# Two fp32 parts of a weight chunk in one tile, a wide product for v, and three full accumulator banks for each branch product in a hybrid encoder trunk

## The chip, the cores and the metric

The kernel runs on one core of a Trainium2 chip. The metric is the device time of one execution in microseconds (us). The kernel before has a median of 2629.47 us over 3 runs (2629.2 to 2629.55). The engines are called by the profile's short names: PE is the matrix engine's multiplications and PEld its weight loads, DVE the vector engine, ACT the scalar engine, POOL the GpSimd engine, SP the engine that issues most transfers. PSUM is the memory that PE writes its sums to; one of its banks holds 512 fp32 numbers in each of 128 partitions.

## The reference

The reference is an encoder trunk of two layers on 256 tokens of width 2048, in fp32:

```python
h = rmsnorm(x, norm1_g[l])
z = h @ w_in[l]               # conformer 2*512 | short conv 3*512 | q,k,v 3*768 | gates 3*2048
y_a = conformer_conv(z) @ w_a_out[l]          # 512 -> 2048
y_b = short_gated_conv(z) @ w_b_out[l]        # 512 -> 2048
y_c = dilated_attention(q, k, v) @ w_c_out[l] # 256 -> 2048
g_a, g_b, g_c = split(sigmoid(zg + b_gate[l]))
m = g_a * y_a + g_b * y_b + g_c * y_c
x = x + m @ w_o[l]
x = x + (silu(h2 @ w_ffn_gate[l]) * (h2 @ w_ffn_up[l])) @ w_ffn_down[l]   # h2 = rmsnorm(x, norm2_g[l])
```

The attention has 12 heads in 3 groups with dilations 1, 4 and 16; the conformer branch has a depthwise convolution with 31 taps and a layer norm. After the last layer comes one more RMSNorm.

## The kernel before, in words

**Every product is made of two parts.** Each fp32 operand is split into a rounded part (type fp32r) and the rest of it: x = hi + lo. A product is hi·hi + lo·hi + hi·lo. In the activations' tiles, 128 x 512, the high part fills the left 256 columns and the rest the right 256. `product` (lines 175 to 193) therefore multiplies the high part of a weight block with all 512 columns at once (line 189, a "wide" product) and the weight's rest with the left 256 (line 190, a "narrow" one). The left and the right half of the bank then have to be added: `joined` (lines 195 to 203) copies the right half to SBUF on ACT (line 198) and adds the two on DVE (line 202).

**Weights come in chunks of 128 x 1024** (1280 for the branches' output weights, 1408 for the second FFN matrix; these are cut in two pieces). There are 1072 pieces. For each piece ACT makes the rounded part `wh` (line 144) and DVE the rest `wl` (line 145). Raw chunks, `wh` and `wl` have three buffers each in the pool `wp`; a piece is split while the two ahead of it are still to be multiplied. A piece of 1024 columns holds 8 weight blocks, so 8 wide and 8 narrow products.

**v is the exception.** For v the activations are the stationary operand and the weights move: lines 499 to 501 make three narrow products for each of the 16 blocks of the depth, 2 halves of the tokens, 3 head groups and 2 layers. Each accumulator `pv` uses 256 of its bank's 512 columns, and one ACT copy (line 506) takes it to SBUF.

**The branch products** (lines 600 to 614) are another: for each of the 16 column blocks j, ten weight blocks make y_a (4), y_b (4) and y_c (2) with three narrow products each (lines 610 to 612). y_a and y_b share one bank (`pab`), y_c has half of another (`pc`). `branch_out` multiplies them with the gates on DVE straight from PSUM (lines 619 to 621), sums them, and splits the sum for the following product with w_o. All accumulators, of every product, come from the pool `pa`, which has five banks; a second pool `px` of three banks serves the attention's and norms' small products.

**What sets the order.** The program is recorded in the order of the Python code, and a list scheduler with its own model of times then places each instruction in the queue of its engine; each engine runs its queue in order. The splits of weight pieces have a higher priority than the rest (`SOONER`). The work beside the products (convolution taps on DVE, layer norm, attention) waits in the queue `beside`, and `some` lets a part of it be recorded after each piece. The layer norm of the conformer branch needs two sums over four tiles on POOL (`ln_sum`, lines 429 to 431), a small product `mu` on PE, and four SiLUs on ACT (line 453); the sigmoids (line 636), SiLUs and exponentials (line 537) each need their function table loaded on ACT when the one before was another. The attention's results `csp` are two tiles; each branch's y_c needs both. The first branch products are recorded after gate product 14, the second after gate product 16 of a layer's 48.

Of the kernel before, what the change touches and what calls it, by code (L numbers as in the profile page):

```python
# [16 lines left out]
P = 128  # L17
# [32 lines left out]
def trunk(ctx, tc, xt, wf, win, wv, wy, wo, wgu, wd, cst, fin, dist, out):  # L50
# [39 lines left out]
    def acc(name):  # L90
        return pa.tile([P, 2 * S], F32, tag="acc", name=name)
# [44 lines left out]
    def split_to(pi):  # L136
        while state["split"] < min(pi, len(pieces)):
            i = state["split"]
            ci, a, b = pieces[i]
            load_to(ci + 1)  # L140
            wh = wp.tile([P, 1024], F32R, tag="wh", name="wh")
            wl = wp.tile([P, 1024], F32R, tag="wl", name="wl")
            with tc.high_priority(SOONER if state["use"] >= 2 else 0):
                nc.scalar.copy(wh[:, :b - a], raws[ci][:, a:b])  # L144
                nc.vector.tensor_sub(wl[:, :b - a], raws[ci][:, a:b], wh[:, :b - a].bitcast(F32))  # L145
            split[i] = (wh, wl)
            if b == chunks[ci][1]:
                del raws[ci]
            state["split"] += 1
# [13 lines left out]
    def drain():  # L163
        some(1e9)

    def piece():
        i = state["use"]
        load_to(min(len(chunks), pieces[min(i + 1, len(pieces) - 1)][0] + AHEAD_LOAD))
        split_to(i + AHEAD_SPLIT)
        state["use"] += 1  # L170
        _, a, b = pieces[i]
        wh, wl = split.pop(i)
        return wh, wl, (b - a) // P

    def product(dst, xs, whole=False, budget=0.9):

# [161 lines left out]
    for k in range(KD):  # L338
        norm.take(k)
        if k < KD - 3:  # L340
            wh, wl = tile2r("wh"), tile2r("wl")
        else:

            wh, wl = (wp.tile([P, 1024], F32R, tag=t, name=t) for t in ("wh", "wl"))
        for a, b in CUTS.get(k, [(0, HEAD * P)]):
            nc.scalar.copy(wh[:, a:b], fw[k][:, a:b])
            nc.vector.tensor_sub(wl[:, a:b], fw[k][:, a:b], wh[:, a:b].bitcast(F32))
        for n, ps in enumerate(heads):
            nc.tensor.matmul(ps, wh[:, n * P:(n + 1) * P], turned(norm.xs[k]), start=k == 0, stop=False)
        for n, ps in enumerate(heads):  # L350
            nc.tensor.matmul(ps[:, :S], wl[:, n * P:(n + 1) * P], turned(norm.xs[k][:, :S]), start=False, stop=k == KD - 1)
# [38 lines left out]
    for l in range(DEPTH):  # L390
# [96 lines left out]
        h = norm.later  # L487
        v = [[None] * 2 for _ in range(NG)]
        for g in range(NG):
            pv = [acc("v")[:, :S] for _ in range(2)]  # L490
            k = 0
            while k < KD:
                wh, wl, nk = piece()
                for i in range(nk // 2):
                    w = slice(i * S, (i + 1) * S)
                    for b in range(2):
                        hi = h[k][:, b * P:(b + 1) * P]
                        lo = h[k][:, S + b * P:S + (b + 1) * P]
                        nc.tensor.matmul(pv[b], hi, turned(wh[:, w]), start=k == 0, stop=False)
                        nc.tensor.matmul(pv[b], lo, turned(wh[:, w]), start=False, stop=False)  # L500
                        nc.tensor.matmul(pv[b], hi, turned(wl[:, w]), start=False, stop=k == KD - 1)
                    k += 1
                some(0.9)
            for b in range(2):
                v[g][b] = vp.tile([P, S], F32, tag=f"v{g}{b}", name="v")
                nc.scalar.copy(v[g][b], pv[b])

# [83 lines left out]
        gates, m = {}, []  # L593

        def branch(j):
            ps = branch_products()
            with tc.high_priority(2 * SOONER if j == KD - 1 else 0):
                branch_out(j, ps)

        def branch_products():  # L600
            ys = asp + bsp + csp
            pab, pc = acc("yab"), acc("yc")[:, :S]
            dsts = [pab[:, :S]] * 4 + [pab[:, S:]] * 4 + [pc] * 2
            first, final = (0, 4, 8), (3, 7, 9)
            k = 0
            while k < 10:
                wh, wl, nk = piece()
                for i in range(nk):
                    w = slice(i * P, (i + 1) * P)
                    nc.tensor.matmul(dsts[k], wh[:, w], turned(ys[k][:, :S]), start=k in first, stop=False)  # L610
                    nc.tensor.matmul(dsts[k], wh[:, w], turned(ys[k][:, S:]), start=False, stop=False)  # L611
                    nc.tensor.matmul(dsts[k], wl[:, w], turned(ys[k][:, :S]), start=False, stop=k in final)
                    k += 1
            return pab, pc

        def branch_out(j, ps):
            pab, pc = ps
            ga, gb, gc = gates.pop(j)
            nc.vector.tensor_mul(ga, ga, pab[:, :S])
            nc.vector.tensor_mul(gb, gb, pab[:, S:])  # L620
            nc.vector.tensor_mul(gc, gc, pc)
            nc.vector.tensor_add(ga, ga, gb)
            nc.vector.tensor_add(ga, ga, gc)
            mj = tile2r("mj")
            halves(mj, ga)
            m.append(mj)
# [166 lines left out]
```

## Time and profile before

| what | us |
|---|---|
| median of the runs | 2629.47 |
| the profiled execution | 2629.61 |
| its span, from the first to the last instruction | 2627.8 |
| PE busy | 2609.8 |
| DVE busy | 1895.1 |
| ACT busy | 1440.4 |
| POOL busy | 117.5 |

The granted clock of PE is 0.998. PE is busy nearly everywhere, so a duration is best read as the distance between the starts of two matmuls: the records overlap, since a matmul of 256 columns is shown with 0.28 us and the next one starts 0.11 us after it. The stages of the first layer stand in the trace in this order: the conformer's inputs, q and k up to 114.4 us, v from there to about 147 us, the short convolution's inputs, the gates from 210.4 us, the branch products among them from 302 us.

### The profile page before, as it was taken

The numbers are of one execution on the slowest core, as the hardware profiler recorded it, in microseconds if no ns is written. First come the engines' busy times: TensorE is split into PE (matmuls) and PEld (weight loads), VectorE is DVE, ScalarE is ACT, GpSimd is POOL, SyncE is SP. The second block draws the span as 40 slices with busy tenths as digits, with TensorE's granted clock in tenths as the row PEclk, the third lists the DMA queues.
The fourth block names the chain that finished last, engine by engine and source line by source line (L and its number), as shares of the span: only waits on it lengthen the run. The fifth ranks groups of instructions, "written<-read, shape, count | busy, mean of one in ns | idle before, by whom it ended". The sixth has DMA issues, their size and how long they took to land.

```text
span 2627.8 us, 42886 instructions
## 1 busy us (share of the span) xinstructions
PE 2609.8 (99%) x16740; PEld 2411.8 (92%) x16740; DVE 1895.1 (72%) x2903; ACT 1440.4 (55%) x2063; POOL 117.5 (4%) x92
## 2 busy tenths in 40 slices
PE   9999999999999999999999999999999999999998
PEld 8998899999999999999999989999999999999997
DVE  8998566678766666666899966666787666666665
ACT  6547655555645545445664565555565454454555
POOL 2001000011000000000102000000200000000002
PEclk9999999999999999999999999999999999999999
DMA  6665466666666666666566555666666666666664
GB/s 239 202 201 186 149 207 197 204 200 200 201 201 201 202 200 202 205 197 204 194 201 200 191 183 171 204 198 199 204 199 202 199 201 205 197 201 203 199 204 154
DMA packets 137581, 519.36 MB, mean 198 GB/s; under 512 B 15520, under 2 KB 17184, under 8 KB 137376
## 3 DMA queue, kind: packets, MB, share of 16 engines
q1 hardware_dynamic: 136368, 515.28, 60.3%
q8 instruction: 131, 2.15, 0.3%
q10 hardware_dynamic: 1008, 1.32, 0.1%
q14 instruction: 74, 0.61, 0.1%
HBM read 514.45 MB, written 2.10 MB: 197 GB/s over the span
## 4 chain that ended last, share of the span: by engine, by line
PE 94%; DVE 3%; issue 1%; ACT 1%; POOL 0%; DMA 0%; SPq 0%; POOLq 0%; ACTq 0%; DVEq 0%
PE fgu L189 22%; PE fgu L190 12%; PE gate L189 12%; PE fd L189 12%; PE gate L190 6%; PE fd L190 6%; PE wo L189 4%; PE qk L189 3%; PE wo L190 2%; DVE ac L423 2%; PE zb L189 2%; PE za L189 1%; PE qk L190 1%; PE yab L610 1%; PE yab L611 1%
## 5 line engine op out<-in xcount | busy, mean ns | idle before, releaser
L145 DVE TENSOR_TENSOR wl<-raw,wh 128x1024 fp32r<-128x1024 f32 (+2 forms) x1072 | 1208.0, 1127 | 619.2 <-ACT wh L144 606.7
L144 ACT CAST wh<-raw 128x1024 fp32r<-128x1024 f32 (+2 forms) x1072 | 1032.0, 964 | 1081.9 <-PE fgu L189 325.2
L189 PE MATMUL fgu<-xs,wh 128*128 128x512 f32 x2688 | 881.1, 382 | 0.0
L190 PE MATMUL fgu<-xs,wl 128*128 128x256 f32 x2816 | 768.2, 273 | 0.0
L189 PEld LDWEIGHTS fgu<-xs,wh 128*128 128x128 f32 x2688 | 508.0, 189 | 70.7
L190 PEld LDWEIGHTS fgu<-xs,wl 128*128 128x128 f32 x2816 | 540.7, 192 | 0.0
L189 PE MATMUL gate<-xs,wh 128*128 128x512 f32 x1440 | 477.5, 383 | 0.0
L189 PE MATMUL fd<-fs,wh 128*128 128x512 f32 x1386 | 454.4, 382 | 0.0
L190 PE MATMUL gate<-xs,wl 128*128 128x256 f32 x1536 | 420.1, 274 | 1.0 <-DVE wl L145 0.9
L190 PE MATMUL fd<-fs,wl 128*128 128x256 f32 x1408 | 383.8, 273 | 0.0
L189 PEld LDWEIGHTS gate<-xs,wh 128*128 128x128 f32 x1440 | 272.2, 189 | 37.7 <-issue 0.9
L190 PEld LDWEIGHTS gate<-xs,wl 128*128 128x128 f32 x1536 | 294.8, 192 | 3.2 <-DVE wl L145 1.6
L189 PEld LDWEIGHTS fd<-fs,wh 128*128 128x128 f32 x1386 | 262.0, 189 | 36.2
L190 PEld LDWEIGHTS fd<-fs,wl 128*128 128x128 f32 x1408 | 270.3, 192 | 0.0
L189 PE MATMUL wo<-mj,wh 128*128 128x512 f32 x512 | 167.6, 382 | 0.0
L282 POOL TENSOR_TENSOR sq<-sq 128x256 f32<-128x256 f32 x59 | 63.6, 1078 | 2163.5 <-ACT sq L277 2163.5
L190 PE MATMUL wo<-mj,wl 128*128 128x256 f32 x512 | 138.9, 273 | 0.0
L189 PE MATMUL zb<-xs,wh 128*128 128x512 f32 x384 | 126.0, 383 | 0.0
L189 PE MATMUL qk<-xs,wh 128*128 128x512 f32 x384 | 125.9, 382 | 0.0
L189 PEld LDWEIGHTS wo<-mj,wh 128*128 128x128 f32 x512 | 96.5, 189 | 13.2
L190 PE MATMUL qk<-xs,wl 128*128 128x256 f32 x384 | 104.3, 273 | 0.0
L423 DVE SCALAR_TENSOR_TENSOR ac<-apad,csb,ac 128x256 f32<-128x256 f32 x240 | 103.9, 482 | 0.0
(175 smaller groups left out, 2997.1 us busy)
## 6 DMA issues: line engine op xcount, KB each, us to landing
raw<-in_wgu SPq DMA_DIRECT2D x352, 512.0 KB, 4.3
raw<-in_win SPq DMA_DIRECT2D x312, 512.0 KB, 3.6
raw<-in_wd SPq DMA_DIRECT2D x128, 704.0 KB, 4.1
raw<-in_wo SPq DMA_DIRECT2D x64, 512.0 KB, 4.3
raw<-in_wy SPq DMA_DIRECT2D x32, 640.0 KB, 4.6
raw<-in_wv SPq DMA_DIRECT2D x24, 512.0 KB, 3.5
fw<-in_wf SPq DMA_DIRECT2D x15, 256.0 KB, 5.4
x<-in_xt SPq DMA_DIRECT2D x7, 256.0 KB, 5.4
```

Of the source, the lines that this page charges most:

```text
L144: nc.scalar.copy(wh[:, :b - a], raws[ci][:, a:b])
L145: nc.vector.tensor_sub(wl[:, :b - a], raws[ci][:, a:b], wh[:, :b - a].bitcast(F32))
L189: nc.tensor.matmul(dst, wh[:, c], turned(x), start=k == 0, stop=False)
L190: nc.tensor.matmul(dst[:, :S], wl[:, c], turned(x[:, :S]), start=False, stop=last)
L282: nc.gpsimd.tensor_add(self.sums[0], self.sums[0], sq)
L423: nc.vector.scalar_tensor_tensor(ac[i], apad[:, i, k:k + S], c(C_CW + i * CK + k), ac[i], op0=OP.mult, op1=OP.add)
L610: nc.tensor.matmul(dsts[k], wh[:, w], turned(ys[k][:, :S]), start=k in first, stop=False)
L611: nc.tensor.matmul(dsts[k], wh[:, w], turned(ys[k][:, S:]), start=False, stop=False)
```

## The change

The two parts of a weight piece lie in one tile of 128 x 2 x 1024 with the tag `w`, still with three buffers. For v the moving operand is a view of both parts: one wide product with the activations' high part makes hi·wh in the left and hi·wl in the right half of the bank, and a narrow one adds lo·wh to the left half. The two halves are then joined with `joined`. The branch products take three full banks and make a wide and a narrow product for each weight block; each of the three outputs is joined into a tile `y`, and the gate is multiplied with that. The last block j = 15 of each layer keeps its three narrow products and two banks.

```diff
@@ split_to
-            wh = wp.tile([P, 1024], F32R, tag="wh", name="wh")
-            wl = wp.tile([P, 1024], F32R, tag="wl", name="wl")
+            both = wp.tile([P, 2, 1024], F32R, tag="w", name="w")
+            wh, wl = both[:, 0], both[:, 1]
...
@@ v
-            pv = [acc("v")[:, :S] for _ in range(2)]
+            pv = [acc("v") for _ in range(2)]
...
-                wh, wl, nk = piece()
+                both, nk = piece(pair=True)
                 for i in range(nk // 2):
-                    w = slice(i * S, (i + 1) * S)
+                    w = both[:, :, i * S:(i + 1) * S].rearrange("p b (h j) -> p b j h", h=2)
...
-                        nc.tensor.matmul(pv[b], hi, turned(wh[:, w]), start=k == 0, stop=False)
-                        nc.tensor.matmul(pv[b], lo, turned(wh[:, w]), start=False, stop=False)
-                        nc.tensor.matmul(pv[b], hi, turned(wl[:, w]), start=False, stop=k == KD - 1)
+                        nc.tensor.matmul(pv[b], hi, w, start=k == 0, stop=False)
+                        nc.tensor.matmul(pv[b][:, :S], lo, w[:, 0], start=False, stop=k == KD - 1)
...
-                nc.scalar.copy(v[g][b], pv[b])
+                joined(v[g][b], pv[b])
...
@@ branch_products
-            pab, pc = acc("yab"), acc("yc")[:, :S]
-            dsts = [pab[:, :S]] * 4 + [pab[:, S:]] * 4 + [pc] * 2
+            if whole:
+                pab, pc = acc("yab"), acc("yc")
+                outs = [pab[:, :S], pab[:, S:], pc[:, :S]]
+            else:
+                outs = [acc("yab") for _ in range(3)]
+            dsts = [outs[0]] * 4 + [outs[1]] * 4 + [outs[2]] * 2
...
-                    nc.tensor.matmul(dsts[k], wh[:, w], turned(ys[k][:, :S]), start=k in first, stop=False)
-                    nc.tensor.matmul(dsts[k], wh[:, w], turned(ys[k][:, S:]), start=False, stop=False)
-                    nc.tensor.matmul(dsts[k], wl[:, w], turned(ys[k][:, :S]), start=False, stop=k in final)
+                    if whole:
+                        nc.tensor.matmul(dsts[k], wh[:, w], turned(ys[k][:, :S]), start=k in first, stop=False)
+                        nc.tensor.matmul(dsts[k], wh[:, w], turned(ys[k][:, S:]), start=False, stop=False)
+                    else:
+                        nc.tensor.matmul(dsts[k], wh[:, w], turned(ys[k]), start=k in first, stop=False)
+                    nc.tensor.matmul(dsts[k][:, :S], wl[:, w], turned(ys[k][:, :S]), start=False, stop=k in final)
...
@@ branch_out
-            nc.vector.tensor_mul(ga, ga, pab[:, :S])
-            nc.vector.tensor_mul(gb, gb, pab[:, S:])
-            nc.vector.tensor_mul(gc, gc, pc)
+            for g, y in zip((ga, gb, gc), ps):
+                nc.vector.tensor_mul(g, g, y if j == KD - 1 else joined(tile1("y"), y))
```

Since the scheduler places the instructions by its own model, the change also moves others. Three places of the new queues are shown. In the new kernel line 145 is still the split's rest, line 204 is the join's addition, line 200 its copy, line 426 a convolution tap, lines 456 and 643 the SiLU and the sigmoid, line 334 the copy in `halves`, lines 191 and 192 the wide and narrow product of `product`, and lines 620 and 621 those of the branches.

The first place is DVE's queue in the v stage of the first layer, over the splits of four pieces. Before, each of these splits is followed by four taps and nothing else.

```order
L145 TENSOR_TENSOR w<-raw,w 128x1024
L426 SCALAR_TENSOR_TENSOR ac<-apad,csb,ac 128x256 x2
L204 TENSOR_TENSOR v<-v,half 128x256
L426 SCALAR_TENSOR_TENSOR ac<-apad,csb,ac 128x256 x2
L145 TENSOR_TENSOR w<-raw,w 128x1024
L204 TENSOR_TENSOR v<-v,half 128x256
L426 SCALAR_TENSOR_TENSOR ac<-apad,csb,ac 128x256 x2
L145 TENSOR_TENSOR w<-raw,w 128x1024
L426 SCALAR_TENSOR_TENSOR ac<-apad,csb,ac 128x256 x4
L145 TENSOR_TENSOR w<-raw,w 128x1024
L426 SCALAR_TENSOR_TENSOR ac<-apad,csb,ac 128x256 x3
```

Two joins stand among the splits of four pieces, and 13 taps in place of 16; the last tap of the first layer comes three splits later than before, and so do the layer norm's steps behind it.

The second place is ACT's queue in the gates of the first layer, where the conformer branch is normalized and activated (`y`) and split (`asp`). Before:

```order
L144 CAST wh<-raw 128x1024
L636 ACT_TABLE_LOAD
L636 ACTIVATE gt<-gt,csb 128x256
L453 ACT_TABLE_LOAD
L453 ACTIVATE y<-y,csb 128x256 x2
L332 CAST asp<-y 128x128x2 x2
L144 CAST wh<-raw 128x1024
L198 COPY half<-gate 128x256
L636 ACT_TABLE_LOAD
L636 ACTIVATE gt<-gt,csb 128x256
L144 CAST wh<-raw 128x1024 x2
```

Now, between one `L144 CAST w<-raw 128x1024` that stands directly ahead of these rows and two that stand directly behind them:

```order
L456 ACT_TABLE_LOAD
L456 ACTIVATE y<-y,csb 128x256
L200 COPY half<-gate 128x256
L456 ACTIVATE y<-y,csb 128x256
L643 ACT_TABLE_LOAD
L643 ACTIVATE gt<-gt,csb 128x256
L456 ACT_TABLE_LOAD
L456 ACTIVATE y<-y,csb 128x256 x2
L334 CAST asp<-y 128x128x2 x2
L643 ACT_TABLE_LOAD
L643 ACTIVATE gt<-gt,csb 128x256
L334 CAST asp<-y 128x128x2 x2
```

All of the branch's activations, with four table loads, now stand between the split of piece 78 and that of piece 79 (counted from 0); before, they were spread over the splits of pieces 75 to 79. In the second layer this part of the queue is as it was.

The third place is PE's queue at the end of the first two branches of the first layer, with buffer numbers. Before, y_c of both branches waits for the second attention tile `csp_3479`, each in a bank of its own:

```order
L612 MATMUL yc_3658<-csp_3173,wl_3660 128x256
L610 MATMUL yc_3508<-csp_3479,wh_3509 128x256
L610 MATMUL yc_3658<-csp_3479,wh_3659 128x256
L611 MATMUL yc_3508<-csp_3479,wh_3509 128x256
L612 MATMUL yc_3508<-csp_3479,wl_3510 128x256
L611 MATMUL yc_3658<-csp_3479,wh_3659 128x256
L612 MATMUL yc_3658<-csp_3479,wl_3660 128x256
L189 MATMUL gate_3707<-xs_695,wh_3680 128x512
```

Now, where `yab_3323` is y_c of the first branch, `yab_3469` y_b and `yab_3470` y_c of the second; `yab_3470` gets the bank that `yab_3323` held, so that its first product waits until `yab_3323` is joined into `y_3362`:

```order
L621 MATMUL yab_3469<-bsp_2351,w_3471 128x256
L620 MATMUL yab_3323<-csp_3293,w_3324 128x512
L621 MATMUL yab_3323<-csp_3293,w_3324 128x256
L620 MATMUL yab_3470<-csp_2995,w_3471 128x512
L621 MATMUL yab_3470<-csp_2995,w_3471 128x256
L620 MATMUL yab_3470<-csp_3293,w_3471 128x512
L621 MATMUL yab_3470<-csp_3293,w_3471 128x256
L191 MATMUL gate_3519<-xs_682,w_3486 128x512
```

The join of `yab_3323` stands behind the split of the piece `w_3522` on ACT (`L144 CAST w_3522<-raw_3484`, then `L200 COPY half_3363<-yab_3323`) and on DVE (`L145 TENSOR_TENSOR w_3522<-raw_3484,w_3522`, then `L204 TENSOR_TENSOR y_3362<-yab_3323,half_3363`); that split takes over the buffer of `w_3324`, which the same product of `yab_3323` is the last to read.

More of the change, by code (lines that the diff above doesn't have):

```diff
@@ L145, in split_to @@
                 nc.vector.tensor_sub(wl[:, :b - a], raws[ci][:, a:b], wh[:, :b - a].bitcast(F32))
-            split[i] = (wh, wl)
+            split[i] = both
             if b == chunks[ci][1]:
@@ L164, in drain, with piece @@
         some(1e9)
-    def piece():
+    def piece(pair=False):
         i = state["use"]
@@ L171, in piece @@
         _, a, b = pieces[i]
-        wh, wl = split.pop(i)
-        return wh, wl, (b - a) // P
+        both = split.pop(i)
+        if pair:
+            return both, (b - a) // P
+        return both[:, 0], both[:, 1], (b - a) // P
     def product(dst, xs, whole=False, budget=0.9):
@@ L342, in trunk @@
         else:
-            wh, wl = (wp.tile([P, 1024], F32R, tag=t, name=t) for t in ("wh", "wl"))
+            both = wp.tile([P, 2, 1024], F32R, tag="w", name="w")
+            wh, wl = both[:, 0], both[:, 1]
         for a, b in CUTS.get(k, [(0, HEAD * P)]):
@@ L595, in branch, with branch_products @@
         def branch(j):
-            ps = branch_products()
+            ps = branch_products(j == KD - 1)
             with tc.high_priority(2 * SOONER if j == KD - 1 else 0):
                 branch_out(j, ps)
-        def branch_products():
+        def branch_products(whole):
             ys = asp + bsp + csp
-            pab, pc = acc("yab"), acc("yc")[:, :S]
-            dsts = [pab[:, :S]] * 4 + [pab[:, S:]] * 4 + [pc] * 2
+            if whole:
[4 more added lines that the diff above has]
+            dsts = [outs[0]] * 4 + [outs[1]] * 4 + [outs[2]] * 2
             first, final = (0, 4, 8), (3, 7, 9)
@@ L609, in branch_products @@
                     w = slice(i * P, (i + 1) * P)
-                    nc.tensor.matmul(dsts[k], wh[:, w], turned(ys[k][:, :S]), start=k in first, stop=False)
-                    nc.tensor.matmul(dsts[k], wh[:, w], turned(ys[k][:, S:]), start=False, stop=False)
-                    nc.tensor.matmul(dsts[k], wl[:, w], turned(ys[k][:, :S]), start=False, stop=k in final)
+                    if whole:
[4 more added lines that the diff above has]
+                    nc.tensor.matmul(dsts[k][:, :S], wl[:, w], turned(ys[k][:, :S]), start=False, stop=k in final)
                     k += 1
-            return pab, pc
+            return outs
         def branch_out(j, ps):
-            pab, pc = ps
             ga, gb, gc = gates.pop(j)
-            nc.vector.tensor_mul(ga, ga, pab[:, :S])
-            nc.vector.tensor_mul(gb, gb, pab[:, S:])
-            nc.vector.tensor_mul(gc, gc, pc)
+            for g, y in zip((ga, gb, gc), ps):
+                nc.vector.tensor_mul(g, g, y if j == KD - 1 else joined(tile1("y"), y))
             nc.vector.tensor_add(ga, ga, gb)
```

## The prediction

> **What bounds the kernel now.** I read the page first, then who waited for whom on PE, then the timeline of single stages.
>
> ```profile
> span 2627.8 us, 42886 instructions
> PE 2609.8 (99%) x16740; PEld 2411.8 (92%) x16740; DVE 1895.1 (72%) x2903; ACT 1440.4 (55%) x2063; POOL 117.5 (4%) x92
> PE 94%; DVE 3%; issue 1%; ACT 1%; POOL 0%; DMA 0%; SPq 0%; POOLq 0%; ACTq 0%; DVEq 0%
> ...
> PE rows L323 <- DVE root L316: 2.3, 1, 2.3
> PE gate L190 <- DVE wl L145: 0.9, 1, 0.9
> ```
>
> PE sets the time: 99% busy, 94% of the chain that ended last, and between the start and the final norm (the 2.3 us) its largest named wait is 0.9 us. The profiled execution took 2629.6 us (span 2627.8 and 1.8 around it), 0.1 over the median of 2629.5. So two things can change the time: the distance from matmul to matmul, and new waits of PE. The kernel's measurements cannot tell a change under 0.2%, 5.3 us, from none.
>
> **The matmuls.** The start times in v, in the first branch product, and in a stage that already uses pairs:
>
> ```profile
> 115.11 0.28 PE L499 MATMUL v<-wh,xs 128*128 128x256 f32 x1
> ...
> 116.45 0.28 PE L499 MATMUL v<-wh,xs 128*128 128x256 f32 x1
> 302.53 0.28 PE L610 MATMUL yab<-asp,wh 128*128 128x256 f32 x1
> ...
> 303.20 0.28 PE L610 MATMUL yab<-asp,wh 128*128 128x256 f32 x1
> 59.64 0.38 PE L189 MATMUL qk<-xs,wh 128*128 128x512 f32 x1
> ...
> 61.93 0.38 PE L189 MATMUL qk<-xs,wh 128*128 128x512 f32 x1
> ```
>
> In v, four triples of narrow products take 116.45 − 115.11 = 1.34 us, 0.335 each; in the branch two take 0.67, the same. Seven pairs of a wide and a narrow one take 2.29, 0.327 each. A pair instead of a triple saves 7.9 ns. Triples replaced: v 2 layers x 3 groups x 16 blocks x 2 halves = 192; branches 2 x 15 x 10 = 300 (j = 15 keeps its own). 492 x 7.9 ns = **−3.9 us**. The columns multiplied stay the same, 768 for each block; only one instruction's overhead goes. A wide product with the weights moving is not in the trace; v's narrow ones, with the weights moving, keep the same distance as the branch's, so I take the pair's 0.327 for it too (bounds: 0.327 and no saving at 0.335, so −3.9 to 0).
>
> The Trainium skill's page "TensorE: Matmul & The Clock Gate", section "Wait — 56ns, not 53.3ns?", gives N / 2.4 GHz + 2.5 ns from start to start: 109.2 ns narrow, 215.8 wide. By that a triple costs 327.5 ns and a pair 325.0, and the saving would be an estimated 1.2 us. The measured triple is slower than the rule has it, and the rows decide.
>
> **What is added off PE.** The joins add 90 copies on ACT (the 12 of v replace 12 others) and 102 additions on DVE:
>
> ```profile
> L198 ACT COPY half<-gate 128x256 f32<-128x256 f32 x90 | 32.8, 365 | 0.0
> L202 DVE TENSOR_TENSOR gt<-gate,half 128x256 f32<-128x256 f32 x90 | 37.6, 418 | 0.4 <-ACT half L198 0.4
> ```
>
> That is 33 us on ACT and 102 x 0.418 = 43 us on DVE, on engines that are 55% and 72% busy. In the branches they hide under the gates' products; without that cover every join chain of 0.37 + 0.42 would show, 30 branches' last ones for 24 us. In v the cover is thin, since DVE is full there:
>
> ```profile
> 120.00:130.00 10.00, 10.00 (x92) 10.00 (x91) 10.00 (x19) 4.62 (x6) 0.00 (x0) 1.00 0.49 170
> 122.57 1.05 ACT L144 CAST wh<-raw 128x1024 fp32r<-128x1024 f32 x1 [1.63 <-PE v L500]
> 125.14 1.21 DVE L145 TENSOR_TENSOR wl<-raw,wh 128x1024 fp32r<-128x1024 f32 x1
> 126.27 1.65 DVE L423 SCALAR_TENSOR_TENSOR ac<-apad,csb,ac 128x256 f32<-128x256 f32 x4
> 127.85 1.21 DVE L145 TENSOR_TENSOR wl<-raw,wh 128x1024 fp32r<-128x1024 f32 x1
> ```
>
> The cast at 122.57 starts when PE begins the piece two ahead of the one being split; its rest is ready at 126.35, and PE reaches it two pieces of 8 x 0.335 = 2.68 later, at about 127.9: 1.5 us in hand. The wide product needs the rest at once, where three narrow ones needed it after 0.22. The new queue has, for four pieces, 4 x 1.13 + 13 taps x 0.395 + 2 joins x 0.33 = 10.3 us on DVE against 32 x 0.327 = 10.5 on PE; the worst single interval, four taps and a join, eats 0.33. So nothing shows, 0 to 0.7 us. The one tile for both parts delays a cast until the last narrow product instead of the last wide one, 0.22 us of the same reserve: 0.
>
> **What the new order moves: the pile on ACT.** In the first layer all of the conformer branch's activations now stand between the casts of pieces 78 and 79. Their prices, from where they stood before:
>
> ```profile
> 229.39 0.36 ACT L198 COPY half<-gate 128x256 f32<-128x256 f32 x1
> 229.66 0.67 ACT L332 CAST asp<-y 128x256 fp32r<-128x256 f32 x1
> 230.11 1.06 ACT L144 CAST wh<-raw 128x1024 fp32r<-128x1024 f32 x1
> 231.20 1.28 ACT L636 ACT_TABLE_LOAD   x1
> 232.49 0.51 ACT L636 ACTIVATE gt<-gt,csb 128x256 f32<-128x256 f32 x1
> 233.02 1.28 ACT L453 ACT_TABLE_LOAD   x1
> 234.31 1.09 ACT L453 ACTIVATE y<-y,csb 128x256 f32<-128x256 f32 x2
> 235.31 1.11 ACT L332 CAST asp<-y 128x256 fp32r<-128x256 f32 x2
> 236.21 1.06 ACT L144 CAST wh<-raw 128x1024 fp32r<-128x1024 f32 x1
> 232.37 1.15 PE L523 MATMUL sc<-qk 64*128 64x256 f32 x12
> 241.41 0.38 PE L189 MATMUL gate<-xs,wh 128*128 128x512 f32 x1
> 242.69 0.38 PE L190 MATMUL gate<-xs,wl 128*128 128x256 f32 x1 [0.89 <-DVE wl L145]
> ```
>
> From start to start a table load takes 1.29, a sigmoid 0.53, two SiLUs 1.00, two splits 0.90, a copy 0.27. The new pile: 4 loads 5.16 + 4 SiLUs 2.0 + 2 sigmoids 1.06 + 4 splits 1.8 + a copy 0.27 = 10.3 us; the largest before was 5.1 (231.20 to 236.21). When cast 78 starts, PE begins piece 76 and has pieces 76 to 78 to do, 3 x 2.62, then 0.22 until it needs the rest of 79, and the attention scores of 1.1 stand between: 9.2 us. The rest of 79 is there after 0.95 + 10.3 + 1.06 + 1.21 = 13.5. PE waits 4.4. Before, it waited at this piece too: 242.69 − 241.41 − 0.22 = 1.06. Term: **+3.3** (bounds 0, if the activations find their turn earlier, and 4.4, if the scores stand elsewhere).
>
> **The bank.** `yab_3470` needs the bank of `yab_3323`, and PE stands in between. Behind the last product of `yab_3323` come its own length 0.28, the cast of piece `w_3522` 1.05, its rest on DVE 1.13, the join's addition 0.42: 2.9, less the 0.11 that PE spends anyway, 2.8 us. Here PE has nothing else: its queue is in order, and the gates' products are behind the waiting one. Before, both y_c had banks, and what PE lost was the wait for a piece's rest:
>
> ```profile
> 324.94 0.38 PE L189 MATMUL gate<-xs,wh 128*128 128x512 f32 x1
> 325.42 0.38 PE L190 MATMUL gate<-xs,wl 128*128 128x256 f32 x1
> ```
>
> 0.48 instead of 0.22. Term: **+2.5** (bounds 0 and 3). Later branches have two or three gate products of 5.2 us between them, and the bank they get was left long before: 0.
>
> **Sum.** 2629.6 − 3.9 + 3.3 + 2.5 + 0.5 (the middle for v, the layer norm's sums and the start) = **2632.0 us**, by the page's matmul rule 2634.7.
>
> **Rivals.** *Hidden after all*: the activations' inputs come earlier on the chip than in the scheduler's model, ACT works them off in its idle time, and the attention is done early enough to free the bank. Then −3.9 alone counts: 2625.7, with one of the waits left about 2628.5. For it: PE lost only 1.06 to a pile of 5.1. Against it: ACT takes its queue in order, and 10.3 us is beyond any stock of three pieces.
>
> *The layer norm's sums* end on the other side. In the first layer `mu` on PE and the last taps on DVE both move by three pieces, so two POOL additions still have to fit between them, beside a full DVE:
>
> ```profile
> 1425.28 17.50 POOL L429 TENSOR_TENSOR lns<-ac 128x256 f32<-128x256 f32 x1 [109.97 <-DVE ac L423]
> 182.48 5.02 POOL L429 TENSOR_TENSOR lns<-ac 128x256 f32<-128x256 f32 x1 [142.04 <-DVE zb L202]
> 203.04 2.72 POOL L430 TENSOR_TENSOR lns<-lns,ac 128x256 f32<-128x256 f32 x1 [15.54 <-DVE ac L423]
> 205.84 1.60 POOL L431 TENSOR_TENSOR lns<-lns,ac 128x256 f32<-128x256 f32 x1
> ```
>
> The same addition took 1.6 to 17.5 us. If these two take 5.0 each instead of 2.72 and 1.60, PE waits 5.7 longer: 2637.7. It decides from about 4.5 us for both on. Against it: DVE's load there is no higher than before. The Trainium skill's page "SBUF — State Buffer", section "Who interferes with whom", says that a DVE instruction with two SBUF inputs contends with a GpSimd instruction that reads SBUF; the 17.5 us beside taps agree.
>
> *The matmul rule*: a triple's extra belongs to the stage, not to the form, and the new pairs cost what the formula says against narrow products likewise; the saving shrinks to 1.2 us: 2634.7.
>
> That the wide products are not made is excluded: the new queue has 192 and 300 of them.
>
> **Chances.** Forecast 0.58, hidden 0.22, sums 0.14, matmul rule 0.06. The range takes in the terms' bounds: 2626.5 to 2636.5. Faster by over 0.2% (under 2624.2) needs the hidden case and a larger saving: 0.05. Slower by over 0.2% (over 2634.7): the sums, most of the rule's 0.06 and the upper end of the forecast: 0.23. Within: 0.72.
>
> **What will show it.** Pairs 0.327 us apart in v and the branches, no narrow triple but at j = 15; one wait of PE of 3 to 5 us at about 240 us in the first layer, ended by a cast or its rest; one of some 2.8 us at the second branch, ended by a join on DVE; none of these in the second layer; PE busy in v. It is wrong if PE waits at every branch (joins that hold banks), or if neither wait is there.

## The result, and the profile after

| | before | after |
|---|---|---|
| median of 15 runs each, same chip | 2629.55 us | 2635.61 us |
| lowest and highest | 2628.41, 2630.15 | 2633.10, 2637.07 |
| the profiled execution | 2629.61 us | 2633.43 us |

The ratio is 1.0022, with a 95% interval of 1.0015 to 1.0029: 6.1 us slower. The interval lies on both sides of the 0.2% that the prediction set as its mark. The time lies within the predicted range, but 3.6 us above the forecast of 2632.0, and 5 of the 15 runs lie above the range's upper end of 2636.5. The runs of the changed kernel fall in two groups, 7 from 2633.1 to 2634.3 and 8 from 2635.6 to 2637.1; the profile below is of an execution of the lower group, and the experiments show what parts them. One run of experiment 1 (7071 us, mean clock 0.46) and one of the kernel before beside it (3895 us, 0.65) were slow as a whole and enter no ratio below.

**The totals.** The page of the changed kernel opens so (busy time, share of the span, instructions):

```profile
span 2631.6 us, 41831 instructions
PE 2609.3 (99%) x16248; PEld 2396.5 (91%) x16248; DVE 1923.2 (73%) x3005; ACT 1461.9 (56%) x2153; POOL 103.1 (4%) x92
```

PE has 492 matmuls fewer, 16740 − 16248, one for each triple that became a pair. DVE has its 102 additions and ACT its 90 copies more. PE's busy time hardly differs, since it covers stretches that run slowly as well as those that run fast; what was lost has to be looked for in places.

**The waits.** Who waited for whom on PE in the changed kernel (us in total, times, longest):

```profile
PE gate L191 <- ACT w L144: 4.0, 2, 3.6
PE yab L620 <- DVE y L204: 2.8, 1, 2.8
```

Both are new. The first ends with a cast on ACT, the second with a join on DVE, as the prediction had it.

**The pairs.** Starts in v and in a branch product of the timeline of PE (start, duration, operation):

```profile
114.16 0.38 PE L502 MATMUL v<-w,xs 128*128 128x512 f32 x1
...
116.46 0.38 PE L502 MATMUL v<-w,xs 128*128 128x512 f32 x1
326.54 0.38 PE L620 MATMUL yab<-bsp,w 128*128 128x512 f32 x1
...
327.19 0.38 PE L620 MATMUL yab<-bsp,w 128*128 128x512 f32 x1
```

Seven pairs of v take 116.46 − 114.16 = 2.30 us, 0.328 each; two of the branch take 0.65, 0.325 each. The wide product with the weights moving costs no more than the other.

**Where the time stands.** The first product of the second layer, before and then after (one timeline each):

```profile
1311.90 0.38 PE L189 MATMUL za<-xs,wh 128*128 128x512 f32 x1
```

```profile
1317.18 0.38 PE L191 MATMUL za<-xs,w 128*128 128x512 f32 x1
```

The first layer ends 5.28 us later, but the span is only 3.8 longer (2631.6 and 2627.8): the second layer gains 1.5 us, of the 1.95 that its half of the pairs is worth. All of the loss is in the first layer.

**The pile.** ACT in the changed kernel between the casts of pieces 78 and 79:

```profile
230.64 1.05 ACT L144 CAST w<-raw 128x1024 fp32r<-128x1024 f32 x1 [1.71 <-PE gate L192]
231.70 1.28 ACT L456 ACT_TABLE_LOAD   x1
...
242.19 2.00 ACT L144 CAST w<-raw 128x1024 fp32r<-128x1024 f32 x2
```

From 231.70 to 242.19 it takes 10.5 us; the sum of prices had 10.3. And PE at the same place:

```profile
239.46 0.27 PE L192 MATMUL gate<-xs,w 128*128 128x256 f32 x1
243.30 0.48 PE L191 MATMUL gate<-xs,w 128*128 128x512 f32 x1 [3.56 <-ACT w L144]
244.24 0.61 PE L191 MATMUL gate<-xs,w 128*128 128x512 f32 x1 [0.46 <-ACT w L144]
244.75 0.58 PE L192 MATMUL gate<-xs,w 128*128 128x256 f32 x1
245.12 0.64 PE L191 MATMUL gate<-xs,w 128*128 128x512 f32 x1
...
245.76 0.64 PE L191 MATMUL gate<-xs,w 128*128 128x512 f32 x1
...
248.00 0.27 PE L192 MATMUL gate<-xs,w 128*128 128x256 f32 x1
```

The narrow product at 239.46 makes room at 239.57. PE then stands for 3.73 us, makes one wide product, stands for 0.72 (243.52 to 244.24), makes another, and goes on at 244.75: up to there 5.18 us for two wide products of 0.22, so 4.74 lost, of which it stood 4.45; the rest is the second wide product, which already takes 0.51. What comes next was in no term. The pairs are now 0.64 us apart (245.12, 245.76) instead of 0.327, until 247.9. From 244.75 to 248.00 there are 3.25 us for five pairs, which take 1.64 elsewhere: 1.6 more lost. The loss at this place is 4.7 + 1.6 = 6.3 us, against 1.06 before. The view by windows names the reason; first the kernel before, then the changed one (columns: window, its length, then busy time and instructions of PE, PEld, DVE, ACT and POOL, then PE's granted clock, the DMA share and GB/s):

```profile
245.00:250.00 5.00, 5.00 (x33) 4.58 (x32) 3.48 (x6) 4.80 (x6) 0.00 (x0) 1.00 0.69 243
```

```profile
245.00:250.00 5.00, 5.00 (x23) 4.48 (x24) 3.40 (x6) 4.96 (x9) 0.00 (x0) 0.71 0.68 210
```

PE is "busy" for all 5.00 us from 245 to 250 but issues 23 matmuls instead of 33: the granted clock is 0.71 over this window. **After the stand the clock runs at half for a few microseconds** (the experiments say for how many), so the stand is paid for a second time.

The Trainium skill has a rule for this, in "TensorE: Matmul & The Clock Gate", section "What's actually happening": a gate passes half of the clock's pulses when PE was idle over an observation window of about 3.4 us, and the full clock comes back after a busy one; the windows run freely, whatever the kernel does. The pairs at 0.64 agree with the half rate. A window without any work was not needed here: the clock falls at 244.46 us, and of the 3.41 us before that PE stood 2.97 and worked for 0.44.

**The bank.** PE, ACT and DVE of the changed kernel at the second branch, from three timelines:

```profile
327.74 0.27 PE L621 MATMUL yab<-csp,w 128*128 128x256 f32 x1
330.83 0.45 PE L620 MATMUL yab<-csp,w 128*128 128x512 f32 x1 [2.82 <-DVE y L204]
```

```profile
328.05 1.04 ACT L144 CAST w<-raw 128x1024 fp32r<-128x1024 f32 x1 [0.27 <-PE yab L621]
```

```profile
327.82 2.54 DVE L145 TENSOR_TENSOR w<-raw,w 128x1024 fp32r<-128x1024 f32 x2 [1.12 <-ACT w L144]
330.27 0.42 DVE L204 TENSOR_TENSOR y<-yab,half 128x256 f32<-128x256 f32 x1
```

The chain is the predicted one: the end of `yab_3323`'s last product at 328.01, a cast, a rest, the join at 330.27, PE at 330.83. The loss is 330.83 − 327.74 − 0.11 = 2.98 us. In this execution the clock stays whole behind it. In others it does not, as the fourth experiment shows.

### The profile page after: what moved, and what is told of

Same layout as the page of the kernel before. It is cut to its first block, busy times and chain, and to the rows that moved or that the text cites. A ratio compares the mean times of both kernels' runs of the same rounds, so it can differ in the third digit from the quotient of the medians.

```text
span 2631.6 us, 41831 instructions
## 1 busy us (share of the span) xinstructions
PE 2609.3 (99%) x16248; PEld 2396.5 (91%) x16248; DVE 1923.2 (73%) x3005; ACT 1461.9 (56%) x2153; POOL 103.1 (4%) x92
## 4 chain that ended last, share of the span: by engine, by line
PE 98%; ACT 1%; DMA 0%; issue 0%; DVE 0%; POOL 0%; SPq 0%; POOLq 0%
PE fgu L191 22%; PE gate L191 12%; PE fgu L192 12%; PE fd L191 12%; PE gate L192 6%; PE fd L192 6%; PE wo L191 4%; PE zb L191 3%; PE qk L191 3%; PE yab L620 3%; PE wo L192 2%; PE za L191 2%; PE v L502 2%; PE qk L192 2%; PE zb L192 2%; PE yab L621 1%
## 5 line engine op out<-in xcount | busy, mean ns | idle before, releaser
L145 DVE TENSOR_TENSOR w<-raw,w 128x1024 fp32r<-128x1024 f32 (+2 forms) x1072 | 1211.7, 1131 | 609.9 <-ACT w L144 606.7
L144 ACT CAST w<-raw 128x1024 fp32r<-128x1024 f32 (+2 forms) x1072 | 1031.7, 964 | 1068.3 <-PE fgu L192 314.9
L191 PE MATMUL fgu<-xs,w 128*128 128x512 f32 x2688 | 881.0, 382 | 0.0
L192 PE MATMUL fgu<-xs,w 128*128 128x256 f32 x2816 | 767.7, 273 | 0.0
L191 PEld LDWEIGHTS fgu<-xs,w 128*128 128x128 f32 x2688 | 507.9, 189 | 70.7
L192 PEld LDWEIGHTS fgu<-xs,w 128*128 128x128 f32 x2816 | 540.7, 192 | 0.1
L191 PE MATMUL gate<-xs,w 128*128 128x512 f32 x1440 | 479.0, 384 | 4.0 <-ACT w L144 4.0
L191 PE MATMUL fd<-fs,w 128*128 128x512 f32 x1386 | 454.4, 382 | 0.0
L192 PE MATMUL gate<-xs,w 128*128 128x256 f32 x1536 | 421.3, 274 | 0.0
L191 PEld LDWEIGHTS gate<-xs,w 128*128 128x128 f32 x1440 | 272.9, 190 | 43.3 <-ACT w L144 4.6
L192 PEld LDWEIGHTS gate<-xs,w 128*128 128x128 f32 x1536 | 295.6, 192 | 2.6 <-issue 1.7
L191 PEld LDWEIGHTS fd<-fs,w 128*128 128x128 f32 x1386 | 262.0, 189 | 36.2
L192 PEld LDWEIGHTS fd<-fs,w 128*128 128x128 f32 x1408 | 270.3, 192 | 0.0
```

The source lines that it names most:

```text
L191: nc.tensor.matmul(dst, wh[:, c], turned(x), start=k == 0, stop=False)
L192: nc.tensor.matmul(dst[:, :S], wl[:, c], turned(x[:, :S]), start=False, stop=last)
```

## The experiments

The theory after the result: the change gains its 3.9 us, and loses by two stands of PE in the first layer, each of which can bring a stretch of slower clock behind it. The main rival: the joins load ACT and DVE everywhere, and the two places are only where that load comes to light; taking them away would move the loss elsewhere. Each ratio is to runs of the kernel before on the same chip, with its 95% interval.

**1. The new v alone** (the branches as before: two banks, narrow triples, no joins):

```diff
-            ps = branch_products(j == KD - 1)
+            ps = branch_products()
...
-                nc.vector.tensor_mul(g, g, y if j == KD - 1 else joined(tile1("y"), y))
+            nc.vector.tensor_mul(ga, ga, pab[:, :S])
...
```

> The one tile and v's wide products with their joins; the branches as before (three narrow products, two banks). If the loss is two waits of PE in the first layer, of which the pile of activations on ACT comes from v's joins on DVE: the pile's wait of some 4.4 us at 240 us and the slow clock behind it (1.9 us) are here, less the 1.06 us that PE waited there before; the saving is 192 x 7.9 ns = 1.5 us; no wait for a bank: about 2629.6 - 1.5 + 5.3 = 2633.4 us. If instead the joins' load on ACT and DVE costs wherever they stand, 12 of 102 joins cost next to nothing and the time is about 2628.5. If the one tile is to blame, this loses as much as the whole change, 2635.

Measured: median 2634.21 us, ratio 1.0017 (1.0008 to 1.0026). The waits and the windows of this kernel:

```profile
PE gate L191 <- ACT w L144: 3.6, 1, 3.6
```

```profile
245.00:250.00 5.00, 5.00 (x17) 4.20 (x18) 3.87 (x8) 4.97 (x7) 0.00 (x0) 0.53 0.63 205
```

The pile is there without any branch join, and no wait for a bank. So it comes from the new v alone; that the shifted taps of the v stage bring it about, by way of the layer norm's steps behind them, is read from the order and was not tried apart. Its runs do not split into two groups; the ten that enter the ratio lie between 2633.7 and 2634.5.

**2. The new branches alone** (v as before):

```diff
-            pv = [acc("v") for _ in range(2)]
+            pv = [acc("v")[:, :S] for _ in range(2)]
...
-                joined(v[g][b], pv[b])
+                nc.scalar.copy(v[g][b], pv[b])
```

> The one tile and the branches' three banks, wide products and joins; v as before (three narrow products, one copy). Two waits: no pile (ACT's queue as before the change, a wait of 1.06 us), saving 300 x 7.9 ns = 2.4, the bank's wait of 2.8 to 3.0 in place of 0.27: about 2629.6 - 2.4 + 2.6 = 2629.8 us, in some executions up to 1.7 more if the clock goes down behind the bank's wait too. If the joins' load costs wherever they stand, 90 of 102 joins are here and with them nearly the whole loss: about 2635. If the one tile is to blame: 2635.

Measured: 2632.48 us, ratio 1.0010 (1.0001 to 1.0019). In its waits there is the bank and no pile:

```profile
PE yab L621 <- DVE y L204: 2.8, 1, 2.8
```

In the profiled execution (2631.52 us) the clock is 1.00 behind this wait. The runs spread from 2630.2 to 2633.8 us, those above 2632.4 with a mean clock of 0.997 and those below with 0.998. The median is 1.0 above the expected upper end of 2631.5.

**3. The one tile alone** (both parts in one tile; v and branches as before):

```diff
-            wh = wp.tile([P, 1024], F32R, tag="wh", name="wh")
-            wl = wp.tile([P, 1024], F32R, tag="wl", name="wl")
+            both = wp.tile([P, 2, 1024], F32R, tag="w", name="w")
+            wh, wl = both[:, 0], both[:, 1]
...
```

> Only the one tile for both parts of a piece; all products, banks and copies as before. Two waits: neither is here, 2629 to 2631 us (the release of one tile instead of two is 0.2 us later, under a reserve of over 1 us). If the one tile is to blame (a cast waits for the last narrow product): most of the loss, about 2635.

Measured: 2630.81 us, ratio 1.0005 (0.9996 to 1.0014). Neither wait is there. Whether the tile costs something like 0.8 us can't be told from these runs. In its trace the first product of the second layer starts at 1311.88 us (1311.90 before), so the loss in the first layer is not the tile's; the 1.1 us by which this span is longer come behind that place.

**4. The changed kernel once more**, unaltered, for a second trace:

> The changed kernel once more, for a second profile. Its executions fall into two groups, 2633.1 to 2634.3 and 2635.6 to 2637.1 us, with a mean clock of 0.997 and 0.996. If the second group is the one in which the clock also goes down behind the bank's wait of 3.0 us: a profile of that group shows a granted clock under 1 at about 330 us beside that at 245 us, and 1.7 to 3 us lost there. If the groups have another cause (the transfers, or PE's start), the difference lies elsewhere in the span.

Measured: 2636.05 us, ratio 1.0023 (1.0014 to 1.0033). This profiled execution belongs to the upper group. PE at the bank, and the windows around both stands:

```profile
331.88 0.77 PE L620 MATMUL yab<-csp,w 128*128 128x512 f32 x1 [2.82 <-DVE y L204]
...
333.29 0.63 PE L191 MATMUL gate<-xs,w 128*128 128x512 f32 x1
...
333.93 0.63 PE L191 MATMUL gate<-xs,w 128*128 128x512 f32 x1
...
335.18 0.38 PE L191 MATMUL gate<-xs,w 128*128 128x512 f32 x1
```

```profile
245.00:250.00 5.00, 5.00 (x18) 4.36 (x18) 3.60 (x6) 4.96 (x8) 0.00 (x0) 0.52 0.61 210
...
330.00:335.00 5.00, 3.12 (x10) 2.70 (x11) 4.61 (x12) 4.97 (x12) 0.00 (x0) 0.67 0.64 199
```

The wait for the bank is the same 2.82 us, to the hundredth, but here pairs 0.64 us apart follow it (333.29, 333.93). From 331.88 to 335.18 five pairs take 3.30 us instead of 1.64, 1.7 us lost. At the pile the slow clock lasts longer, to 249.8 us instead of 247.9 (0.52 in the window instead of 0.71), for another 0.9. Together 2.6 us: that is about the distance of the two traces (spans 2634.3 and 2631.6) and of the two groups. **The same wait costs 3.0 us in one execution and 4.7 in another.**

What parts the two can be read from windows of 0.1 us: where the clock changes within one, its mean lies between 0.5 and 1 and says when. First the changed kernel's first profile, then this one:

```profile
244.40:244.50 0.10, 0.10 (x1) 0.03 (x1) 0.10 (x1) 0.08 (x2) 0.00 (x0) 0.82 0.00 0
247.80:247.90 0.10, 0.10 (x2) 0.10 (x2) 0.10 (x1) 0.10 (x1) 0.00 (x0) 0.61 0.93 123
```

```profile
249.80:249.90 0.10, 0.10 (x2) 0.10 (x2) 0.00 (x0) 0.10 (x1) 0.00 (x0) 0.97 0.01 0
331.70:331.80 0.10, 0.00 (x0) 0.00 (x0) 0.10 (x2) 0.10 (x1) 0.00 (x0) 0.63 0.93 369
```

The clock falls at 244.46 and is whole again at 247.88, 3.41 us later. In this profile it returns at 249.81 and falls again at 331.73: 81.92 us, 24 times 3.413. All the changes found in this way fit: the slow stretches of the first layer last 3.41 or 6.83 us in the six profiles that have one, and from each profile's last return to its fall near the end it is a whole number of times 3.413 us (695 times in the first profile, to 2620.14). So the clock changes only at boundaries 3.41 us apart, and where they lie differs between two executions of the same kernel. At the bank, PE stands for 2.84 us of the period that ends at 331.73 here (from 328.89 on), and the clock falls. In the first profile the boundary at 329.80 divides the stand (327.85 to 330.83) into 1.95 and 1.03 us, in experiment 2 the one at 326.56 into 2.14 and 0.84, and it does not fall. So in these profiles it is the place of the stand between the boundaries that decides whether the wait is paid twice; that this also parts the groups of runs without a profile is an inference from their times.

**5. The pile broken up, the bank left** (the SiLU as y times its sigmoid, so that it needs no table of its own):

```diff
-            nc.scalar.activation(y, y, AF.Silu, scale=c(C_LG + i), bias=c(C_LB + i))
+            sg = tile1("sg")
+            nc.scalar.activation(sg, y, AF.Sigmoid, scale=c(C_LG + i), bias=c(C_LB + i))
+            nc.vector.tensor_scalar(y, y, c(C_LG + i), c(C_LB + i), op0=OP.mult, op1=OP.add)
+            nc.vector.tensor_mul(y, y, sg)
```

> The changed kernel, but the conformer module's SiLU is formed as y times its sigmoid (Sigmoid on ACT, the scale and shift and the product on DVE), so that no other table is loaded there; the result is the same. The loads of tables, 1.29 us each, go out of ACT's pile between the casts of pieces 78 and 79 of the first layer: four of them, 5.1 us, more than the 4.45 us that PE waited there. Theory (two waits of PE, each with a drop of the clock behind it): the first wait and its 1.9 us of half clock go, 6.3 us, the bank's wait of 2.8 us stays: about 2636.0 - 6.3 = 2629.7 us, and no slice below 0.9 of the clock about 245 us. Rival (the joins' own load on DVE and ACT makes the loss everywhere, the pile only shows where it ends): a wait of 2 us or more comes back at another product within 20 us, and the time stays above 2633.

Measured: 2629.34 us, ratio 0.9999 (0.9990 to 1.0008); expected was 2629.7. No wait for `gate` is left among PE's. ACT's timeline shows that the edit did more than take loads away:

```profile
236.31 1.07 ACT L144 CAST w<-raw 128x1024 fp32r<-128x1024 f32 x1
...
237.73 0.58 ACT L457 ACTIVATE sg<-y,csb 128x256 f32<-128x256 f32 x1
...
238.91 1.07 ACT L144 CAST w<-raw 128x1024 fp32r<-128x1024 f32 x1
```

No table is loaded, and the scheduler now puts the casts of weight pieces between the activations. So the run shows what the pile was worth, not how much of that is the four loads and how much the order. The bank's wait is still there, 2.8 us, and in this profile with the slower clock behind it (nine of the 11 runs lie from 2628.9 to 2629.9 us and two at 2627.4 and 2627.6; two executions without that stretch would fit, but none was profiled):

```profile
325.00:330.00 5.00, 5.00 (x21) 4.41 (x21) 4.69 (x12) 3.40 (x6) 0.00 (x0) 0.66 0.59 189
```

**6. The bank's wait away, the pile left** (the first two branches of each layer with two banks and triples, as j = 15):

```diff
-            ps = branch_products(j == KD - 1)
+            ps = branch_products(j in THREES)
...
-                nc.vector.tensor_mul(g, g, y if j == KD - 1 else joined(tile1("y"), y))
+                nc.vector.tensor_mul(g, g, y if j in THREES else joined(tile1("y"), y))
...
+THREES = (0, 1, KD - 1)
```

> The changed kernel, but the first two branch outputs of each layer are formed as before (two banks, narrow products in triples, no joins), as the last one is in the change; all else stays. Theory: the branch tile that stood on its bank's release at 327 us takes no joined bank, so that wait of 2.8 to 3.0 us goes, and with it the second drop of the clock that part of the runs have; the pile's wait at 240 us stays with its drop. 24 more triples in place of pairs cost 24 x 7.9 ns = 0.2 us. About 2636.0 - 1.7 (the drop) - 2.8 + 0.2 = 2631.7 us, in one group of times and not in two 2.5 us apart. Rival (the bank's wait only moves to the third branch): a wait of 2 us or more on a joined bank shows up to 40 us later, and the time stays at 2634 to 2636.

Measured: 2632.39 us, ratio 1.0012 (1.0003 to 1.0021), against an expected 2631.7. No joined bank is waited for any more. Ten of the 11 runs lie from 2632.1 to 2633.9 and one at 2631.0.

**7. Both edits together:**

> The two edits of the runs beside it together: the SiLU by way of the sigmoid, and the first two branch outputs of each layer as before. Theory: neither wait is left and the pairs' 3.9 us stand: 2629.6 - 3.9 + 0.2 = 2625.9 us, and about 1 us less than that if the SiLU's edit by itself takes away the 1.06 us that PE waited at the pile before the change. Rival (what the joins cost lies elsewhere too): no less than the kernel before, 2629 or more.

Measured: 2625.31 us (2624.93 to 2626.74), ratio 0.9985 (0.9977 to 0.9994): faster than the kernel before. Expected was 2625.9 or up to 1 less. Its page's line of busy times and its largest wait:

```profile
PE 2606.8 (99%) x16288; PEld 2398.4 (91%) x16288; DVE 1923.8 (73%) x3009; ACT 1452.4 (55%) x2136; POOL 102.8 (4%) x92
```

```profile
PE rows L325 <- DVE root L318: 2.3, 1, 2.3
```

All of v's joins and 78 of the 90 branch joins are still in it, and DVE is as busy as in the changed kernel. With the two places gone, the loss does not come back elsewhere. The rival of the joins' own load falls.

**8. The SiLU's edit in the kernel before**, as a control (the diff of experiment 5 on line 453):

> The kernel before with the SiLU as y times its sigmoid, and nothing else: what that edit is worth without the change. Theory: PE's 1.06 us at the pile goes and nothing else moves, 2629.6 - 1.1 = 2628.5 us (2628 to 2629.6). If it gains more than 2 us, the table loads cost something at other places as well, and the gain of the two runs with this edit isn't the pile's alone.

Measured: 2628.07 us, ratio 0.9995 (0.9986 to 1.0004), where 2628.5 was expected. So of the 4.3 us between experiment 7 and the kernel before, 1.5 is this edit's own, by the medians. The rest of the change, without its two stands, is worth 2628.07 − 2625.31 = 2.8 us. Its pairs are worth 452 x 7.9 ns = 3.6 us: 40 triples came back (16288 − 16248 matmuls; the expectation of experiment 6 counted 24). Where the other 0.8 us are, these runs don't show.

**9. A smaller pile** (experiment 7, with the old SiLU for two of the four tiles):

```diff
-            sg = tile1("sg")
+            if i > 1:
+                sg = tile1("sg")
...
+            else:
+                nc.scalar.activation(y, y, AF.Silu, scale=c(C_LG + i), bias=c(C_LB + i))
```

> As the kernel with both edits, but the first two of the four SiLUs of each layer are left as they were, with their own table; so two of the pile's four loads are back. By the pile's sum (4.45 us waited, less 2 x 1.29) PE should wait about 1.9 us there in all, with products in between, where the change has 4.45 in nearly one piece. Theory (the clock falls only behind a stand of about 3 us or more, as behind the waits of 2.8 and 3.7 us): no slice below 0.95 of the clock, and 1 to 2.5 us more than the kernel with both edits, 2626.5 to 2628. Rival (any stand of PE over about 1 us lowers the clock for some 3 us behind it): 1.7 us more than that for each stand, 2629 or more, and a granted clock of 0.5 to 0.9 in the slices from 245 to 255 us.

Measured: 2628.71 us, ratio 0.9998 (0.9988 to 1.0007). Its waits and windows:

```profile
PE gate L192 <- DVE w L145: 1.9, 3, 0.9
...
PE zb L192 <- DVE w L145: 1.5, 1, 1.5
```

```profile
240.00:245.00 5.00, 3.89 (x22) 3.02 (x21) 5.00 (x12) 3.51 (x6) 0.00 (x0) 1.00 0.30 105
245.00:250.00 5.00, 4.44 (x27) 4.09 (x28) 4.11 (x7) 4.09 (x7) 0.00 (x0) 1.00 0.61 187
```

At the pile the expected 1.9 us are waited, in pieces of 0.9 and less, and the clock stays at 1.00 in this profile: here the stands are paid once. The time is 0.7 above what the theory gave, and the edit brought a wait of 1.5 us at another place, `zb`, that no theory had: 1.9 + 1.5 = 3.4 is about the distance to experiment 7 (3.4 by the medians, 3.9 when each is taken against the kernel before on its own chip, 2629.08 and 2629.61).

**10. A shorter wait for the bank** (the changed kernel, with the branches further apart):

```diff
-BRANCHES = {max(3 * n + 2, 14 + n * 11 // 5): n for n in range(KD)}
+BRANCHES = {max(3 * n + 2, 16 + n * 31 // 15): n for n in range(KD)}
```

> The changed kernel with the branch blocks spaced wider at the start of each layer's gates (block n after gate product max(3n + 2, 16 + 31n/15) in place of the spacing before), so that more products lie between the first branch's last product and the second branch's demand for a bank. The pile stays. Theory (the bank's wait is the chain of 2.8 us less what PE does in between): it shrinks to 0.5 to 2 us, and since no stand of 2.8 us is left there, no second drop of the clock: 2631.5 to 2633.5 us in one group. Rival (the wait moves to another branch): 2.8 us at a later branch, and times of 2633 to 2637 in two groups as before.

Measured: 2632.58 us, ratio 1.0012 (1.0003 to 1.0021), within the expected 2631.5 to 2633.5. The wait for the bank, the timeline of PE there and the window behind it:

```profile
PE yab L620 <- DVE y L204: 1.6, 1, 1.6
```

```profile
337.39 0.27 PE L621 MATMUL yab<-bsp,w 128*128 128x256 f32 x1
339.28 0.45 PE L620 MATMUL yab<-csp,w 128*128 128x512 f32 x1 [1.62 <-DVE y L204]
...
340.66 0.48 PE L191 MATMUL gate<-xs,w 128*128 128x512 f32 x1 [0.48 <-DVE gt L204]
...
341.50 0.64 PE L191 MATMUL gate<-xs,w 128*128 128x512 f32 x1
342.14 0.64 PE L191 MATMUL gate<-xs,w 128*128 128x512 f32 x1
```

```profile
340.00:345.00 5.00, 4.52 (x18) 3.81 (x17) 5.00 (x13) 4.05 (x6) 0.00 (x0) 0.66 0.81 249
```

PE has more to do meanwhile and waits for the bank 1.6 us instead of 2.8. That half of the theory holds. The other half, that only a stand of 2.8 us or more lowers the clock, falls: the clock is 0.66 in the window from 340 us, and pairs are 0.64 apart from 341.50. PE stood 1.78 us (337.50 to 339.28) and 0.65 more (340.01 to 340.66), 2.4 us out of the 3.2 before it went on; 2.03 of them lie in the 3.41 us before the clock falls at 341.31. So it isn't the length of one stand that decides. The runs lie in two groups, three from 2630.6 to 2631.0 and eight from 2632.4 to 2633.9. Their distance of some 2.2 us is somewhat more than one such stretch (1.7), but which of the stretches the faster runs lack was not profiled.

## Why the prediction was right, and where it fell short

- **The pairs** (−3.9): right. Pairs are 0.325 to 0.328 us apart in v and in the branches. The *matmul rule* as a rival falls with it: the triples before cost 0.335 at the same places.
- **The joins off PE** (0, at most 0.7 in v): right. In v of the changed kernel PE is busy for all of its window beside a full DVE:

```profile
120.00:130.00 10.00, 10.00 (x63) 9.22 (x62) 10.00 (x19) 4.37 (x7) 0.00 (x0) 1.00 0.58 193
```

- **The pile**: the mechanism, the place and the stand were right (10.5 us of work against 10.3 forecast; PE lost 4.7 up to its first narrow product against 4.4, with 0.3 of the slow clock in it). The term of +3.3 is what was wrong. Its step "the rest of 79 is there after 13.5. PE waits 4.4" ended at the moment when PE starts again, and let it go on at 0.327 a pair. It goes on at 0.64. Measured, the place costs 6.3 us in the first trace and 7.2 in the second, so +5.3 to +6.2 over the 1.06 before. The upper bound of 4.4 was too low for the same reason.
- **The bank** (+2.5): the chain and the stand were right, 2.98 − 0.27 = 2.7. Missing is again the slower clock, 1.7 us, in some executions.
- **What the trace of before had shown.** The missing term was there to be read. At the end of the kernel before, where PE waits 2.3 us for the final norm between a few small products, the window says:

```profile
2615.00:2620.00 5.00, 1.22 (x4) 0.93 (x4) 2.94 (x15) 0.37 (x1) 1.19 (x2) 0.54 0.00 0
```

  The clock is 0.54 there, at no cost, because hardly any product follows. It falls at 2615.4, some 0.6 us into that wait, and PE had stood for 0.8 us shortly before, so the 2.3 us are not its only cause. The prediction took 2.3 us from this place as a wait and did not look at its clock; with it, every stand of 2 us or more would have carried a stretch at half clock as its upper bound.
- **The sum by measured terms**: 2629.6 − 3.9 + 5.3 + 2.7 = 2633.7 for the lower group (2633.1 to 2634.3), and 2629.6 − 3.9 + 6.2 + 2.7 + 1.7 = 2636.3 for the upper one (2635.6 to 2637.1). By layers the terms fit less well: for the first they give 6.05 us of loss where 5.28 were measured, for the second 1.95 of gain where it was 1.5; the two differences partly cancel in the total.
- **The layer norm's sums** did not come: no wait for `mu` is in the list of the changed kernel. POOL's second addition took 1.6 and 1.9 us, not 5 (columns: least, median and most in ns, first and last start):

```profile
L433 POOL TENSOR_TENSOR lns<-lns,ac x2: 1584/1748/1913, 208.0 to 1480.8; 128x256 f32<-128x256 f32 x2
```

- **Hidden after all** did not come either: ACT worked its queue in order, and both waits stand in every profile of the changed kernel.
- **The chances**: 0.72 was given to "within 0.2%" and 0.23 to slower. The measured 0.22% lies on that border. With the clock's part in the sum the forecast would have been 2634 to 2636, and slower the likelier side. Nor did the range take in the terms' bounds, as the prediction says: added up they reach from 2625.7 to 2637.7, and the range from 2626.5 to 2636.5.

Open stays how much the one tile costs by itself (0.8 us by the medians, with an interval that takes in zero), and why the second layer gains 1.5 us and not the 1.95 of its pairs.

## What to carry to other kernels

A saving on the bounding engine that is made by more work on its helpers is decided at the few places where the helpers' queues come in bursts, not by their mean load: look for the longest stretch between two deliveries to the bounding engine. Price a stand of PE of 2 us or more with the slow stretch that may follow it, which added 0 or 1.7 us to a stand of 3.0 and 1.6 to 2.4 to one of 4.5 here. This change paid once two small edits, one at each place, had kept PE from standing.

## What the runs showed of the hardware that was not expected

- Behind the pile's stand the granted clock falls to about half in all five profiles that have it (the changed kernel twice, experiments 1, 6 and 10). It ends 4.6 to 6.3 us after PE starts again, at a loss of 1.6 to 2.4 us. One period of 3.41 us at half clock costs about half of it, 1.6 to 1.7 here. Where the clock fell 0.5 to 0.9 us before PE went on (experiments 1, 4, 6 and 10), it took two periods to return; where it fell 1.2 us after PE went on (the first profile) or 0.15 before (the bank in experiment 4), it took one.
- Behind the bank's wait of 2.82 us it falls in two profiles (experiments 4 and 5) and not in two others (the first of the changed kernel, experiment 2); behind stands of 1.78 and 0.65 us close together it falls in experiment 10. So a stand can lower the clock though it is shorter than the 3.4 us that the Trainium skill names in "TensorE: Matmul & The Clock Gate", section "HAM oscillation — how this bites in real kernels", as the gap to avoid. Nor is it the share of one 3.41 us period alone: 2.03 us in two pieces were enough in experiment 10, 2.14 in one piece were not in experiment 2. Where the limit lies the runs don't tell.
- PE's busy share does not show such a stretch: it reads 5.00 of 5.00 us at a clock of 0.52 to 0.71. The count of matmuls in a window and the granted clock do.
